# How the lower parts of the second MLP's weights are made: VectorE's subtraction, or ScalarE's negated copy and an accumulating DMA

## The chip, the cores and the metric

One core of one Trainium2 chip runs the whole program. The metric is the device time of one execution in microseconds (us). Before the change it is 1009.81 us, the median of 3 runs that lie between 1009.17 and 1010.68.

## The reference

A trunk of two layers runs over 512 tokens of width 1024, in float32. What matters here is its last part, the MLP of layer 1 and the final norm:

```
def squared_relu_mlp(h, w1, w2):          # w1: 1024 x 4096, w2: 4096 x 1024
    return jnp.square(jax.nn.relu(h @ w1)) @ w2

h = rms_norm(x, norm_w[1, 1]) * (1 + scale) + shift
x = x + gate * squared_relu_mlp(h, mlp_w1[1], mlp_w2[1])
return rms_norm(x, final_norm_w)
```

Everything ahead of it (attention and MLP of layer 0, the pooling mixer of layer 1) is the same before and after the change.

## The kernel before

Every matrix product is computed from split operands. A float32 matrix W is written as W = hi + lo: hi is W rounded to the type float32r, in which TensorE multiplies, and lo = W - hi is rounded to the same type. A product a @ W is then three matmuls into one PSUM bank: hi by hi, hi by lo, lo by hi. So each weight tile must be loaded, cast by ScalarE (tile `wh`, the upper part) and subtracted (tile `wl`, the lower part) before TensorE may use it. `mm3` (L368) multiplies in the order upper by upper, upper weight by lower activation, lower weight by upper activation; `product` (L1612) takes the lower weight second.

The last stage, from about 670 us on, computes the MLP of layer 1. It consists of two kinds of work on TensorE.

An up block (`up_blocks`, L449) makes 128 of the 4096 hidden columns for all 512 tokens: 24 matmuls of 128x512, about 5.6 us. Two neighbouring blocks share two weight tiles of 128x1024, one for the first four and one for the last four of the eight chunks of the inner dimension. These tiles are loaded by `load_w` (L340), which calls `load_hi` (L346): a DMA from SyncE's queue into a raw tile, the cast by ScalarE at L364, and the subtraction by VectorE at L366.

The down projection is done in Strassen's manner: the hidden columns come in four pairs of 512-column chunks, and for the first three pairs (class `Pair`, L1575) the product with the 2x2 blocks of w2 is replaced by seven products of half the size (`product`, L1612), each of 24 matmuls in two banks, about 5.5 us. Their weight operands are the blocks 11, 21, 22 and the differences T1 to T4, which `combine` (L1600) makes on VectorE in place, on top of the raw tiles of blocks that are split already. `split` (L1587) makes upper and lower parts of one operand: four times a cast of 128x512 by ScalarE (L1595) and a subtraction by VectorE (L1596), in two pairs of tiles of 1024 columns. The last pair is multiplied directly (`direct`, L1680), with four splits.

TensorE's instructions stand in the order written (`TE` is `_InOrder` in this stage). After the loop that starts at L1742 the order for each of the three pairs is: up blocks and product 1, more up blocks, products 2, 5 and 6, up block 0 of the next chunk, product 3, up block 1, product 7, up block 2, product 4, up block 3. The instructions of ScalarE, VectorE, GpSimd and SyncE are placed by a list scheduler, which simulates a timeline; each engine then executes its own in the order placed.

The tiles are few. The pool `wsplit` holds four `wh` and four `wl` tiles, thus the operands of two products; splits and the first two up blocks of a chunk (`pools[0]`) take turns in it. The pool `wsplit2` holds two of each for the last two up blocks of a chunk (`pools[1]`) and the split activations (`split_g`). A cast can start only when TensorE has done with the tile's old content, so the time from that release to the first use of the new content is all that cast and subtraction have. Raw tiles are freed, for the next load on SyncE's queue, when cast and subtraction have read them.

In this stage GpSimd executes nothing. Its queue can issue DMAs, as SyncE's does.

Of the kernel before, what the change touches and what calls it, by code (L numbers as in the profile page):

```python
# [11 lines left out]
F32 = mybir.dt.float32  # L12
# [3 lines left out]
ALU = mybir.AluOpType  # L16
# [68 lines left out]
def trunk(ctx: ExitStack, tc: tile.TileContext, ins, out):  # L85
    nc = tc.nc
    V, S, G, TE = nc.vector, nc.scalar, nc.gpsimd, nc.tensor
# [16 lines left out]
    def nm(s):  # L104
        uid[0] += 1
        return f"{s}_{uid[0]}"
# [71 lines left out]
    rt = wraw.tile([P, RAW], F32, tag="raw", name="rel")  # L178
# [153 lines left out]
    def load(dst, src):  # L332

        if isinstance(V, _InOrder):
            anchor[0] = Q.dma_start(dst, src)
        else:
            with tc.issue_after(anchor[0].ins):
                nc.sync.dma_start(dst, src)

    def load_w(src, a, b, parts=1, lo=V, pool=None):  # L340

        w, make_lo = load_hi(src, a, b, parts, pool)
        make_lo(lo)
        return w

    def load_hi(src, a, b, parts=1, pool=None):  # L346

        n = a * b
        rt = wraw.tile([P, RAW], F32, tag="raw", name=nm("w"))
        if parts == 1:  # L350
            load(rt[:, :n].rearrange("p (a b) -> p a b", a=a), src)
        else:
            dst = rt[:, :n].rearrange("p (a c b) -> p a c b", a=a, c=parts)
            for i in range(parts):
                load(dst[:, :, i], src[:, :, i])
        if pool is None:
            pool = wsplit
        if spare:
            turn[0] += 1
            if turn[0] % 6 >= 4:  # L360
                pool = spare[0]
        th = pool.tile([P, RAW], F32R, tag="wh", name=nm("wh"))
        tl = pool.tile([P, RAW], F32R, tag="wl", name=nm("wl"))
        S.copy(th[:, :n], rt[:, :n])  # L364
        w = tuple(t[:, :n].rearrange("p (a b) -> p a b", a=a) for t in (th, tl))
        return w, lambda e: e.tensor_tensor(tl[:, :n], rt[:, :n], th[:, :n].bitcast(F32), op=ALU.subtract)  # L366

    def mm3(ps, wh, wl, ah, al, start, stop):  # L368
# [8 lines left out]
    class Mlp:  # L377
# [51 lines left out]
        def load_first(self, fp, k0):  # L429
            self.first[fp, k0], lo = load_hi(self.w1[:, k0 : k0 + 4, 256 * fp : 256 * fp + 256], 4, 256)  # L430
            return lo
# [17 lines left out]
        def up_blocks(self, c, g, f0=0, pools=(None, None)):  # L449

            hh, hl = self.h
            for f in range(f0, 4):
                if f % 2 == 0:
                    by = []
                    for k0 in (0, 4):
                        c0 = c * FC + f * P
                        wh, wl = load_w(self.w1[:, k0 : k0 + 4, c0 : c0 + 256], 4, 256, pool=pools[f // 2])
                        by += [(wh, wl, i) for i in range(4)]
                ps = mm_ps()
                cs = slice(f % 2 * P, (f % 2 + 1) * P)  # L460
                for k in range(ND):
                    wh, wl, kk = by[k]
                    mm3(ps, wh[:, kk, cs], wl[:, kk, cs], hh[k], hl[k], k == 0, k == ND - 1)
                self.act(g, f, slice(0, T), ps)
                yield
# [8 lines left out]
        def down(self, c, g):  # L474
            gh, gl = g
            for j in range(ND):
                if j % 2 == 0:
                    wh, wl = load_w(self.w2[:, 4 * c : 4 * c + 4, j * P : j * P + 256], 4, 256)
                ps = mm_ps()
                cs = slice(j % 2 * P, (j % 2 + 1) * P)  # L480
                for f in range(4):
                    mm3(ps, wh[:, f, cs], wl[:, f, cs], gh[:, f], gl[:, f], f == 0, f == 3)
                x_update(j, ps, self.gate[:, j : j + 1])
# [111 lines left out]
    V, S, G, TE = [_InOrder(tc, e) for e in (V, S, G, TE)]  # L595
# [290 lines left out]
    class Attention(Steps):  # L886
# [61 lines left out]
        def load(self, key, src, a, b, parts=1):  # L948
            self.w[key], lo = load_hi(src, a, b, parts)
            yield  # L950
            lo(G)
            yield
# [383 lines left out]
    V, S, G, TE = nc.vector, nc.scalar, nc.gpsimd, nc.tensor  # L1336
# [187 lines left out]
    V, S, G, TE = [_InOrder(tc, e) for e in (V, S, G, TE)]  # L1524
# [13 lines left out]
    V, S, G, TE = nc.vector, nc.scalar, nc.gpsimd, nc.tensor  # L1538
# [12 lines left out]
    for tb in range(NT):  # L1551
        rt = wraw.tile([P, RAW], F32, tag="raw", name=nm("xT"))
# [22 lines left out]
    class Pair:  # L1575
# [11 lines left out]
        def split(self, key, pool=wsplit):  # L1587

            w = []
            for f in range(4):  # L1590
                if f % 2 == 0:
                    th = pool.tile([P, RAW], F32R, tag="wh", name=nm("wh"))
                    tl = pool.tile([P, RAW], F32R, tag="wl", name=nm("wl"))
                cs = slice(f % 2 * T, (f % 2 + 1) * T)
                S.copy(th[:, cs], self.raw[key, f])  # L1595
                V.tensor_tensor(tl[:, cs], self.raw[key, f], th[:, cs].bitcast(F32), op=ALU.subtract)  # L1596
                w.append((th[:, cs], tl[:, cs]))
            return w

# [136 lines left out]
                    V.tensor_tensor(t, p, q, op=op)  # L1736

    gs1 = mlp1.gs
    TE, pools = _InOrder(tc, nc.tensor), (wsplit, wsplit2)
    pair = Pair(0, gs1, True)  # L1740
    blocks = mlp1.up_blocks(1, gs1[1], 2, pools)
# [25 lines left out]
    V, weights = _InOrder(tc, nc.vector), []  # L1767
# [43 lines left out]
```

## Time and profile before

| | us |
|---|---|
| median of the three timed runs | 1009.81 |
| the profiled execution | 1007.54 |
| its span, from first to last instruction | 1005.8 |
| TensorE busy within the span | 972.7 |
| VectorE busy | 702.2 |
| ScalarE busy | 478.6 |
| GpSimd busy | 187.3 |
| mean granted TensorE clock, as a share of 2.4 GHz | 0.992 |

The engines appear as PE (TensorE), DVE (VectorE), ACT (ScalarE), POOL (GpSimd) and SP (SyncE). A line such as L366 is a line of the kernel; L81 is the helper that records instructions whose order is fixed, so there the tile names tell which instruction it is. An engine that is idle does no harm unless the engine that sets the end waits for it. For idle time, the name behind the arrow is the instruction whose end released the waiting one.

### The profile page before, as it was taken

The page shows a single profiled execution, that of the slowest core. Times are in us where ns is not written, and L with a number is a line of the kernel's source. Part 1 is how long each engine was busy: PE and PEld are TensorE (multiplying, and loading weights), DVE is VectorE, ACT ScalarE, POOL GpSimd, SP SyncE. Part 2 cuts the span into 40 slices and gives each one's busy share as a digit, 9 for nine tenths or more (in the row PEclk, how much of TensorE's full clock was granted, in tenths as well). Part 3 has the DMA queues.
Part 4 walks back from the last instruction along what each step waited for, and adds up shares of the span by engine and source line. Part 5 has one row for each costly group of instructions (what it writes and reads, how often), then busy time and mean ns, then how long its engine had stood idle before and what let it go on. Part 6 is the DMA issues. An engine that isn't in the chain of part 4 may idle for free.

```text
span 1005.8 us, 14329 instructions
## 1 busy us (share of the span) xinstructions
PE 972.7 (97%) x5392; PEld 808.6 (80%) x5392; DVE 702.2 (70%) x1192; ACT 478.6 (48%) x886; POOL 187.3 (19%) x136
## 2 busy tenths in 40 slices
PE   6989999998999999999999999899999999989996
PEld 5668888788978778777787999898788788778885
DVE  3679886657885766666574457869658966887485
ACT  6566656656542333334143435574664544344411
POOL 0043335466020111112022337200000000000000
PEclk9999999999999999999999999899999999999999
DMA  9963667542385646556575312181351243043212
GB/s 309 334 170 105 174 189 225 154 140 64 107 256 166 220 134 209 185 169 210 167 224 152 105 44 85 39 294 46 126 167 43 84 161 90 0 146 105 71 35 83
DMA packets 119367, 145.57 MB, mean 145 GB/s; under 512 B 5782, under 2 KB 86018, under 8 KB 119298
## 3 DMA queue, kind: packets, MB, share of 16 engines
q1 hardware_dynamic: 119138, 144.59, 46.4%
q8 instruction: 42, 0.69, 0.3%
q14 instruction: 27, 0.22, 0.1%
q10 hardware_dynamic: 160, 0.07, 0.0%
HBM read 140.25 MB, written 4.39 MB: 144 GB/s over the span
## 4 chain that ended last, share of the span: by engine, by line
PE 81%; DVE 8%; DMA 3%; issue 3%; ACT 2%; POOL 2%; SPq 1%; DVEq 0%; POOLq 0%; ACTq 0%
PE mm L81 32%; PE sc L81 10%; PE mm L370 9%; PE mm L372 9%; PE mm L371 9%; PE po L81 5%; PE tp L81 4%; DMA adaw<-in_ada_w 3%; PE ad L81 2%; DVE hl L81 1%; DVE wl L366 1%; DVE wl L1596 1%; SPq L81 1%; DVE sl L1609 1%; POOL wl L81 1%
## 5 line engine op out<-in xcount | busy, mean ns | idle before, releaser
L364 ACT CAST wh<-w 128x1024 fp32r<-128x1024 f32 x82 | 85.8, 1050 | 110.3 <-PE mm L371 80.5
L81 PE MATMUL mm<-hh,wl 128*128 128x512 f32 (+1 forms) x312 | 117.1, 383 | 4.3 <-DVE wl L366 4.3
L81 PE MATMUL mm<-hl,wh 128*128 128x512 f32 (+1 forms) x312 | 116.7, 381 | 1.6 <-DVE hl L81 1.6
L81 PE MATMUL mm<-hh,wh 128*128 128x512 f32 (+1 forms) x312 | 117.9, 385 | 0.0
L366 DVE TENSOR_TENSOR wl<-w,wh 128x1024 fp32r<-128x1024 f32 x76 | 100.0, 1322 | 23.5 <-ACT wh L364 22.3
L81 POOL TENSOR_TENSOR wl<-w,wh 128x1024 fp32r<-128x1024 f32 x36 | 88.1, 2456 | 77.9 <-ACT wh L81 75.1
L372 PE MATMUL mm<-hh,wl 128*128 128x512 f32 (+1 forms) x256 | 95.8, 375 | 0.0
L371 PE MATMUL mm<-hl,wh 128*128 128x512 f32 (+1 forms) x256 | 95.7, 375 | 0.0
L370 PE MATMUL mm<-hh,wh 128*128 128x512 f32 (+1 forms) x256 | 95.4, 377 | 0.0
L1595 ACT CAST wh<-w 128x512 fp32r<-128x512 f32 x100 | 56.9, 619 | 59.9 <-PE mm L81 24.4
L370 PE MATMUL mm<-gh,wh 128*128 128x512 f32 x192 | 76.0, 396 | 0.1
L371 PE MATMUL mm<-gl,wh 128*128 128x512 f32 x192 | 74.9, 390 | 0.0
L372 PE MATMUL mm<-gh,wl 128*128 128x512 f32 x192 | 74.9, 390 | 0.0
L81 PEld LDWEIGHTS mm<-hh,wl 128*128 128x128 f32 x312 | 59.8, 192 | 18.0 <-DVE wl L366 6.3
L395 ACT ACTIVATE r<-mm 128x512 f32<-128x512 f32 (+1 forms) x46 | 26.8, 583 | 93.5 <-PE mm L81 49.7
L81 PEld LDWEIGHTS mm<-hl,wh 128*128 128x128 f32 x312 | 59.9, 192 | 13.2 <-DVE hl L81 1.8
L81 PEld LDWEIGHTS mm<-hh,wh 128*128 128x128 f32 x312 | 59.9, 192 | 11.8 <-ACT wh L364 0.8
L1596 DVE TENSOR_TENSOR wl<-w,wh 128x512 fp32r<-128x512 f32 x84 | 54.1, 684 | 15.1 <-ACT wh L1595 15.1
L248 DVE SCALAR_TENSOR_TENSOR acc<-adaw,sc,acc 128x512 f32<-128x512 f32 x60 | 46.6, 777 | 20.7 <-DMA adaw<-in_ada_w 20.1
L274 POOL TENSOR_TENSOR adaw<-adaw 128x512 f32<-128x512 f32 x12 | 15.7, 1307 | 233.7 <-ACT adaw L272 225.8
L375 DVE SCALAR_TENSOR_TENSOR x<-mm,mod,x 128x512 f32<-128x512 f32 x48 | 35.6, 746 | 32.0 <-PE mm L372 31.7
L399 DVE TENSOR_TENSOR r<-r 128x512 f32<-128x512 f32 (+1 forms) x49 | 34.4, 703 | 31.5 <-ACT gh L396 31.5
(486 smaller groups left out, 2536.6 us busy)
## 6 DMA issues: line engine op xcount, KB each, us to landing
w<-in_mlp_w SPq DMA_DIRECT2D x98, 512.0 KB, 4.2
adaw<-in_ada_w SPq DMA_DIRECT2D x92, 512.0 KB, 4.6
w<-in_mlp_w SPq DMA_DIRECT2D x64, 256.0 KB, 3.7
w<-in_attn_w_in SPq DMA_DIRECT2D x8, 512.0 KB, 3.9
w<-in_attn_w_out SPq DMA_DIRECT2D x8, 512.0 KB, 3.6
w<-in_attn_w_in SPq DMA_DIRECT2D x8, 392.0 KB, 8.2
xin<-in_x SPq DMA_DIRECT2D x4, 512.0 KB, 5.8
adaw<-in_ada_w SPq DMA_DIRECT2D x8, 256.0 KB, 6.2
```

What stands on the lines that cost most here:

```text
L81: return lambda *args, **kw: self.tc.keep_in_program_order(f(*args, **kw))
L248: V.scalar_tensor_tensor(acc, rv, sk, acc, op0=ALU.mult, op1=ALU.add)
L364: S.copy(th[:, :n], rt[:, :n])
L366: return w, lambda e: e.tensor_tensor(tl[:, :n], rt[:, :n], th[:, :n].bitcast(F32), op=ALU.subtract)
L370: TE.matmul(ps, wh, ah, start=start, stop=False)
L371: TE.matmul(ps, wh, al, start=False, stop=False)
L372: TE.matmul(ps, wl, ah, start=False, stop=stop)
L375: V.scalar_tensor_tensor(x[j][:, ts], ps, g, x[j][:, ts], op0=ALU.mult, op1=ALU.add)
L395: S.activation(r, ps, AF.Relu)
L399: V.tensor_tensor(r, r, r, op=ALU.mult)
L1595: S.copy(th[:, cs], self.raw[key, f])
L1596: V.tensor_tensor(tl[:, cs], self.raw[key, f], th[:, cs].bitcast(F32), op=ALU.subtract)
```

## The change

From the last stage on, the lower part is made in two other steps. ScalarE writes the negated upper part into the lower part's tile (`S.mul` by -1), and a DMA issued from GpSimd's queue adds the raw tile onto it (`accum_op=ALU.add`): the DMA reads the raw tile and the lower tile, both in on-chip memory, and writes the lower tile. VectorE's subtraction at L366 and L1596 disappears there. This holds for the 26 weight tiles of the up blocks (128x1024, 512 KB each) and the 100 of the splits (128x512, 256 KB each). The splits of activations (`split_g`, `act_parts`) and all stages ahead keep their subtractions.

```
+    lo_by_dma = []
+
+    def subtract_by_dma(lo, raw, hi):
+
+        S.mul(lo, hi.bitcast(F32), -1.0)
+        G.dma_start(lo, raw, accum_op=ALU.add)
+
...
         w = tuple(t[:, :n].rearrange("p (a b) -> p a b", a=a) for t in (th, tl))
+        if lo_by_dma:
+            return w, lambda e: subtract_by_dma(tl[:, :n], rt[:, :n], th[:, :n])
         return w, lambda e: e.tensor_tensor(tl[:, :n], rt[:, :n], th[:, :n].bitcast(F32), op=ALU.subtract)
...
                 S.copy(th[:, cs], self.raw[key, f])
-                V.tensor_tensor(tl[:, cs], self.raw[key, f], th[:, cs].bitcast(F32), op=ALU.subtract)
+                subtract_by_dma(tl[:, cs], self.raw[key, f], th[:, cs])
                 w.append((th[:, cs], tl[:, cs]))
...
     gs1 = mlp1.gs
+    lo_by_dma.append(1)
     TE, pools = _InOrder(tc, nc.tensor), (wsplit, wsplit2)
```

## Rows read from the trace of the kernel before

**Rows 1.** The page's first part: each engine's busy time, its share, its instructions.

```profile
PE 972.7 (97%) x5392; PEld 808.6 (80%) x5392; DVE 702.2 (70%) x1192; ACT 478.6 (48%) x886; POOL 187.3 (19%) x136
```

**Rows 2.** Windows of the last stage: busy time by engine, granted clock, DMA share, GB/s.

```profile
670.00:755.00 85.00, 83.97 (x421) 70.38 (x421) 59.49 (x97) 50.77 (x89) 0.00 (x0) 1.00 0.42 133
755.00:925.00 170.00, 165.20 (x712) 132.68 (x711) 134.65 (x215) 76.14 (x117) 0.00 (x0) 1.00 0.30 93
```

**Rows 3.** What TensorE waited for from 670 us: total us, times, longest us.

```profile
PE mm L81 <- DVE wl L366: 4.3, 4, 2.2
PE mm L81 <- DVE gl L400: 1.5, 3, 0.5
```

**Rows 4.** ScalarE's instructions from 670 us by line and shape.

```profile
L1595 ACT CAST wh<-w 128x512 fp32r<-128x512 f32 x100 | 56.9, 619 | 59.9 <-PE mm L81 24.4 <-PE po L81 23.0 <-PE sc L81 11.7
L364 ACT CAST wh<-w 128x1024 fp32r<-128x1024 f32 x26 | 27.2, 1052 | 17.3 <-PE mm L81 9.0 <-PE po L81 4.4 <-issue 2.0
```

**Rows 5.** VectorE's instructions from 670 us by line and shape.

```profile
L1596 DVE TENSOR_TENSOR wl<-w,wh 128x512 fp32r<-128x512 f32 x84 | 54.1, 684 | 15.1 <-ACT wh L1595 15.1
L366 DVE TENSOR_TENSOR wl<-w,wh 128x1024 fp32r<-128x1024 f32 x26 | 31.5, 1219 | 9.9 <-ACT wh L364 9.9
```

**Rows 6.** The DMA issues: queue, count, KB each, median us from issue to landing.

```profile
w<-in_attn_w_in SPq DMA_DIRECT2D x8, 392.0 KB, 8.2
...
x_scratch<-xT SPq DMA_DIRECT2D x4, 512.0 KB, 2.9
...
out<-x SPq DMA_DIRECT2D x6, 256.0 KB, 2.0
bias<-bias_scratch SPq DMA_DIRECT2D x8, 128.0 KB, 6.3
```

**Rows 7.** The page's groups: GpSimd's subtraction of the same shape, earlier in the kernel.

```profile
L81 POOL TENSOR_TENSOR wl<-w,wh 128x1024 fp32r<-128x1024 f32 x36 | 88.1, 2456 | 77.9 <-ACT wh L81 75.1
```

**Rows 8.** ScalarE's timeline, five stretches: start, us, instruction, count, idle before and releaser.

```profile
708.20 1.14 ACT L1595 CAST wh<-w 128x512 fp32r<-128x512 f32 x2
...
716.62 1.05 ACT L364 CAST wh<-w 128x1024 fp32r<-128x1024 f32 x1 [0.82 <-PE sc L81]
...
719.14 1.05 ACT L364 CAST wh<-w 128x1024 fp32r<-128x1024 f32 x1
...
731.07 1.14 ACT L1595 CAST wh<-w 128x512 fp32r<-128x512 f32 x2
...
739.55 2.19 ACT L364 CAST wh<-w 128x1024 fp32r<-128x1024 f32 x2 [0.77 <-PE po L81]
...
886.58 1.06 ACT L364 CAST wh<-w 128x1024 fp32r<-128x1024 f32 x1 [0.79 <-PE sc L81]
```

**Rows 9.** TensorE's timeline, five stretches, same columns.

```profile
714.56 0.39 PE L81 MATMUL sc<-wl,sh 128*128 128x512 f32 x1
...
718.99 0.51 PE L81 MATMUL mm<-hh,wl 128*128 128x512 f32 x1 [0.53 <-DVE wl L366]
...
737.54 0.39 PE L81 MATMUL tp<-wl,sh 128*128 128x512 f32 x1
...
743.97 0.40 PE L81 MATMUL mm<-hh,wl 128*128 128x512 f32 x1
...
890.58 0.51 PE L81 MATMUL mm<-hh,wl 128*128 128x512 f32 x1 [2.15 <-DVE wl L366]
...
894.05 0.50 PE L81 MATMUL mm<-hh,wl 128*128 128x512 f32 x1 [0.42 <-DVE wl L366]
```

**Rows 10.** TensorE's timeline ahead of a spell at the lower clock.

```profile
230.62 0.70 PE L81 MATMUL ad<-sqsum,inv_d 128*128 128x256 f32 x2 [2.65 <-DVE mod L81]
```

**Rows 11.** Windows after that idle time, and in a shorter one late in the kernel.

```profile
231.30:234.80 3.50, 3.50 (x19) 3.50 (x18) 1.79 (x5) 2.21 (x6) 1.77 (x1) 0.51 0.19 32
...
890.60:894.00 3.40, 3.03 (x12) 2.16 (x12) 3.40 (x5) 0.00 (x0) 0.00 (x0) 1.00 0.53 156
```

## The prediction

> **What bounds the kernel now.** I read the page's engine line first. TensorE is busy 972.7 us, 97% of the span, VectorE 70% [rows 1]. The change touches the stage from 670 us on alone, so I read that stage by windows: TensorE is busy 83.97 of 85 and 165.20 of 170 us up to 925, at the full granted clock, while VectorE is busy 59.49 and 134.65, ScalarE 50.77 and 76.14, GpSimd not at all [rows 2]. So TensorE's instruction stream sets the end, and it is idle some 5.8 us in these 255. The list of its waits says for what: 4.3 us for the subtraction of the up blocks' weights (L366), 1.5 us for lower activations (L400), nothing else [rows 3]. All that a faster or an emptier VectorE can give back is therefore 5.8 us. What the change can take is larger, because it lengthens the way from a released weight tile to a lower part that is ready, and that way is already the one on which TensorE waits.
>
> **What goes and what comes.** VectorE loses 84 subtractions (54.1 us), 26 large ones (31.5 us) [rows 5] and 16 more of the small kind near the end (16 by 684 ns, 10.9 us): some 96 us of an engine that is not the bound. By itself I cost that at nothing; TensorE hides it. ScalarE gains as many instructions as it has casts there: 100 of 0.62 us and 26 of 1.05 us [rows 4], taking the multiplication to last as long as the cast of the same shape (two small ones in a row take 1.14 us, so they start 0.52 apart [rows 8]); the casts occupy 56.9 + 27.2 us, so some 84 us more. A third of that falls into the first window, which goes from 51 to about 79 of 85 us: nearly full, so its other work will queue there. I cost that queueing at 0 with an upper bound of 5 us. GpSimd's queue gains 126 DMAs, 39.8 MB, each behind a wait for ScalarE's multiplication; behind the waiting DMA stand only others of its kind, for which TensorE waits.
>
> The new step is the landing time of an accumulating DMA, L. No row shows one. The nearest: a plain store of 256 KB lands 2.0 us after issue, one of 512 KB after 2.9 us [rows 6], so 256 KB more cost 0.9 us and 1.1 are fixed. An accumulation reads two streams and writes one; I count its bytes twice: 1.1 + 2 x 0.9 = 2.9 us for 256 KB, 1.1 + 4 x 0.9 = 4.7 for 512 KB. What GpSimd spends on issuing one is not shown either: I bound it by 0 and by the 2.46 us that it takes to subtract such a tile itself [rows 7], and take the middle, 1.2. That makes L = 4.1 us (256 KB) and 5.9 us (512 KB). The bounds are 2.0 and 2.9 us below (as cheap as the plain stores) and 6.3 and 8.2 us above (the slowest DMAs of this kernel, smaller than these [rows 6]).
>
> The Trainium skill (DMA: Bandwidth & Descriptors, section on the anatomy of one DMA on the SWDGE path) gives for a DMA issued from GpSimd about 2.0 us plus bytes at 436 GB/s, an estimate of 2.6 and 3.2 us; and in Collectives: The Full Stack, section on the bandwidth ceiling, it says that a reduction halves the rate, since it needs two source reads and not because the addition costs cycles. With the bytes doubled the page's line gives 3.2 and 4.4 us, and the sum below would be some 26 us by it instead of 41; no row here shows a DMA from GpSimd, so neither is confirmed.
>
> Now place by place, where the released tile is used soon. **(a) Up block 0 after product 6, three times.** In the first pair the cast starts at 716.62 and ends at 717.67 [rows 8]; TensorE uses the lower part at 718.99, after waiting 0.53 us [rows 9]. After: cast end 717.67, multiplication to 718.72, landing at 724.6: 5.6 us later. The second tile's cast (719.14) slides by the inserted multiplication to 720.19, is negated by 722.3 and lands at 728.2; TensorE, resuming at 724.6, needs it twelve matmuls later (2.8 us), at 727.4: 0.8 us more. Together 6.4. In the third pair the cast ends at 887.64, the landing is at 894.6 where TensorE went on at 890.58, 4.0 us; its second wait of 0.42 us at 894.05 is replaced by one of about 0.3: 3.9. The middle pair lies between, 5.2. Sum 15.5 us.
>
> **(b) Up block 2, three times.** Its second tile is cast as the second of a burst that starts at 739.55 and ends at 741.74 [rows 8]; the lower part is used at 743.97 without a wait [rows 9]: 2.23 us of slack, and the same within 0.1 us in the other two pairs. Its own multiplication takes 1.05 of them, and that of the burst's first tile 0 to 1.05, depending on the order placed; 0.65 remain: 5.9 - 0.65 = 5.25 us each, 15.8 in all.
>
> **(c) Product 6 on T2, three times.** The fourth cast ends at 709.34 [rows 8]; with three multiplications ahead (3 x 0.52) and its own it is negated by 711.5 and lands at 715.6, by 0.5 later if GpSimd issues four in a row; TensorE wants it at 714.56 [rows 9]. That is 1.5 us; I take 1 in each pair, as the casts come some tenths earlier in the others: 3. **(d) Product 7 on T3, three times.** The fourth cast ends at 732.21 [rows 8]; ahead of it stand three small multiplications and a large one, so 735.4, landing 739.8 with the queue; wanted at 737.54 [rows 9]: 2.3 us, 2 per pair, 6. The last split, for block 22 near the end, is like (c): 1. The other splits and tiles are cast a whole product or more ahead of their use, and 24 matmuls of about 0.23 us, 5.5 us, hide most of L.
>
> Two waits move rather than arise. `combine` overwrites raw tiles in place, so on VectorE it now waits for the DMA that reads them; behind it in VectorE's order stand the differences and lower activations that TensorE wants a few us later. With 96 us freed I cost this at 0, bounded by 2 us a pair. SyncE's loads into such tiles are issued some 4 us later; they feed operands that are cast at least an up block later, so nothing.
>
> The direct sum is 15.5 + 15.8 + 3 + 6 + 1 = 41 us. **The clock.** After 2.65 us without a matmul [rows 10] the granted clock was 0.51 for the next 3.5 us, in which TensorE ran at 1.2 instead of 2.4 GHz; after the 2.15 us late in this stage [rows 9] it stayed at 1.00 [rows 11]. The six waits of (a) and (b) are 4 to 6 us long, above both. At half the rate for 3.5 us each loses 1.7 us: 10 us. If none of them drops the clock, 0. I take 10.
>
> The profiled execution took 1007.54 us, 2.3 below the median of the runs. 1007.5 + 41 + 10 = 1058.5; put at the median, 1061 us. With the lower bounds of L the places give 6.6 + 6.8 + 0.2 = 13.6 us and no clock spell: 1023. With the upper ones 22.5 + 22.7 + 9.5 + 12.5 + 3 = 70 us, and 20 of clock over twelve waits: 1100.
>
> **Rivals.** *The DMA is light.* Landings near 3 us, waits too short for the clock: 1023 to 1040. For it speak the 2.0 and 2.9 us of the stores, against it the second stream and GpSimd's part. The line of the Trainium skill's page DMA: Bandwidth & Descriptors, with the bytes counted once, would put it here (an estimate of some 16 us, 1026).
>
> *GpSimd's queue or the accumulation's rate becomes the bound.* If issuing one takes 2.5 us, the bound of rows 7, bursts of four stretch to 10 us: (a) 19.5, (b) 23.9, (c) three times 5.9, (d) three times 7.3, end 6, together 89, and 22 us of clock over thirteen waits: 1120. It decides from about 2.7 us per DMA on, when 126 of them fill the whole 336 us; beyond that the time grows without a limit that the trace shows. Against it: nothing else stands in that queue, and the 16 engines are busy only 42% and 30% of these windows [rows 2].
>
> *All of it is hidden and TensorE gains.* The wait on VectorE (5.8 us) goes and nothing replaces it: 1004. It decides where the landing takes less than the subtraction did, 1.2 us minus the added multiplication's 1.05, thus below about 0.2 us in (a) and 2.2 in (b); no DMA of the kernel lands that fast. Between, at L about 1.5 us, is no change.
>
> **How the numbers follow.** The forecast's case 0.60, the heavy queue 0.22, the light DMA 0.13, hidden or even 0.05 (0.03 faster, 0.02 the same). A measurement of this kernel can tell a difference of about 0.2%, 2 us. Slower: 0.60 + 0.22 + 0.13 = 0.95. The range reaches from the light case, 1025, to the heavy one, 1118, and leaves out what is lighter than the plain stores and a DMA rate below what any row shows.
>
> **What would show it.** Right: in the profile after, TensorE's longest waits are for DMAs into `wl`, at up blocks 0 and 2 with 4 to 6 us, at products 6 and 7 with 1 to 2; granted clock below 1.00 behind the long ones; VectorE's busy time down by about 96 us, ScalarE's up by 84; landings of the new DMAs near 4 and 6 us. Wrong: landings below 3 us or above 9, a GpSimd queue that is never idle, TensorE waiting for ScalarE or for `combine` instead, or a clock that stays at 1.00 through waits of 5 us.

## The result, and the profile after

The changed kernel takes 1115.31 us (median of 4 runs, 1113.89 to 1115.86) against 1009.49 (1007.59 to 1010.68): the ratio is 1.1046, with a 95% interval of 1.1026 to 1.1067. The forecast was 1061. The sign was right and the time lies in the range, but the loss is 106 us where 51.5 were forecast.

The page of the changed kernel: busy time and share, then two of the DMA queues (packets, MB, share of 16 engines), two groups of part 5, and the new DMAs in part 6 (KB each, median us from issue to landing).

```profile
PE 1002.1 (90%) x5392; PEld 823.2 (74%) x5392; DVE 614.4 (55%) x1066; ACT 553.1 (50%) x1012; POOL 296.2 (27%) x262
...
q1 hardware_dynamic: 119138, 144.59, 41.9%
q0 software_dynamic: 18144, 39.85, 20.3%
...
L345 POOL DMA_DIRECT2D wl<-w x126 | 108.8, 1037 | 318.8 <-ACT wl L344 249.9
...
L344 ACT ACTIVATE wl<-wh 128x512 fp32r<-128x512 f32 (+1 forms) x126 | 84.5, 713 | 0.2
...
wl<-w POOLq DMA_DIRECT2D x100, 256.0 KB, 5.4
...
wl<-w POOLq DMA_DIRECT2D x26, 512.0 KB, 7.0
```

Against [rows 1], TensorE's busy time rose by 29.4 us for the same 5392 matmuls; as its instructions are the same, that is the lower clock. VectorE lost 88 us (96 were forecast), ScalarE gained 74.5 on the page (84.5 in the new group itself; instructions in a row overlap by some 0.1 us, as two casts of 0.62 do in [rows 8]). The queue q0 holds the accumulating DMAs alone: 39.85 MB in 20.3% of 16 engines' 1113.2 us is 11.0 GB/s per engine; q1, which copies, moved 19.4.

What TensorE waited for from 670 us on (us in total, times, longest), which before came to 5.8 us in all [rows 3]:

```profile
PE mm L81 <- DMA wl<-w: 53.8, 7, 9.7
PE tp L81 <- DMA wl<-w: 14.5, 5, 4.9
PE sc L81 <- DMA wl<-w: 9.8, 12, 2.3
PE mm L81 <- DVE gl L409: 4.5, 3, 2.8
```

`mm` with `wl` are the up blocks, `tp` product 7, `sc` product 6. The sum, 82.6 us, less the 5.8 of before, is 76.8; with 29.4 us of slower matmuls it accounts for 106.2 of the 107.4 us by which the span grew. TensorE's own timeline of the changed kernel shows the places (start, duration, in brackets the idle time before and its releaser):

```profile
728.62 0.50 PE L81 MATMUL sc<-wl,sh 128*128 128x512 f32 x1 [2.26 <-DMA wl<-w]
741.65 0.80 PE L81 MATMUL mm<-hh,wl 128*128 128x512 f32 x1 [7.50 <-DMA wl<-w]
...
766.78 0.50 PE L81 MATMUL tp<-wl,sh 128*128 128x512 f32 x1 [4.69 <-DMA wl<-w]
...
859.72 0.79 PE L81 MATMUL mm<-hh,wl 128*128 128x512 f32 x1 [8.13 <-DMA wl<-w]
...
884.15 0.79 PE L81 MATMUL tp<-wl,sh 128*128 128x512 f32 x1 [4.91 <-DMA wl<-w]
...
902.40 0.79 PE L81 MATMUL mm<-hh,wl 128*128 128x512 f32 x1 [7.73 <-DMA wl<-w]
```

These are the four places of the prediction. Behind the up blocks' waits the first matmul lasts 0.80 us where it lasted 0.40 to 0.51 [rows 9]; behind the two waits of 2.26 and 4.69 us it still lasts 0.50. In all, the waits of the three pairs are: up block 0 7.50 + 8.13 + 8.76 = 24.4 us (4.3 of them were there before [rows 3]), up block 2 9.65 + 7.73 + 8.54 = 25.9, product 7 14.5, product 6 8.7; the splits near the end wait 1.1. Two that the prediction did not have are 3.5 at the first up block of the stage (from 687.6) and 3.0 more for lower activations.

Windows of the changed kernel (length; busy PE, PEld (TensorE's weight loads), DVE, ACT, POOL; granted clock, DMA share, GB/s): the two of [rows 2], two bursts of lower parts, and the first matmuls of up block 0 behind its wait.

```profile
670.00:755.00 85.00, 67.67 (x316) 55.12 (x315) 29.29 (x52) 48.99 (x88) 20.94 (x24) 0.88 0.75 171
755.00:925.00 170.00, 131.05 (x510) 101.74 (x509) 45.59 (x76) 91.64 (x147) 46.45 (x54) 0.89 0.81 178
...
755.50:785.70 30.20, 15.74 (x60) 11.61 (x58) 0.42 (x1) 17.25 (x28) 10.31 (x12) 0.87 1.01 223
...
838.70:859.70 21.00, 10.31 (x41) 6.81 (x39) 6.56 (x8) 11.61 (x17) 8.61 (x10) 0.91 1.01 226
...
742.00:744.00 2.00, 2.00 (x6) 1.52 (x6) 0.00 (x0) 0.00 (x0) 0.00 (x0) 0.50 0.97 226
```

The column to look at is the last but one, the DMA share. Before, the 16 DMA engines were busy 42% and 30% of these windows [rows 2]; now 75% and 81%, and in the bursts they are full (1.01). GpSimd, which issues, is busy 34% and 41% of a burst: the engines are the limit, not the issuing. The records of one burst, the one behind product 2 of the second pair (GpSimd's DMAs alone, all of 256 KB, us):

```
issued    landed    issue to landing
838.75    842.08    3.33
839.29    843.60    4.31
839.88    845.21    5.34
840.41    847.57    7.15
842.55    849.65    7.10
844.02    851.72    7.70
845.58    853.31    7.73
846.12    855.40    9.28
```

Issues are some 0.5 us apart in the first four, landings 1.5 to 2.4; from 842.22 on, SyncE's loads (256 KB, landing after 5.6 to 7.5) lie between them. Of all 100 small DMAs the shortest landing is 3.28 us, the median 5.4; of the 26 large ones 4.55 and 7.0. Sixteen of the 126 land after more than 9 us, which the prediction had named as a sign of being wrong.

### The profile page after: what moved, and what is told of

Read it like the earlier page. It is cut to its first block, busy times and chain, and to the rows that moved or that the text cites. A ratio compares the mean times of both kernels' runs of the same rounds, so it can differ in the third digit from the quotient of the medians.

```text
span 1113.2 us, 14667 instructions
## 1 busy us (share of the span) xinstructions
PE 1002.1 (90%) x5392; PEld 823.2 (74%) x5392; DVE 614.4 (55%) x1066; ACT 553.1 (50%) x1012; POOL 296.2 (27%) x262
## 3 DMA queue, kind: packets, MB, share of 16 engines
q0 software_dynamic: 18144, 39.85, 20.3%
## 4 chain that ended last, share of the span: by engine, by line
PE 58%; DMA 16%; issue 12%; DVE 7%; POOL 4%; ACT 2%; SPq 0%; POOLq 0%; DVEq 0%; ACTq 0%
PE mm L81 22%; DMA wl<-w 10%; PE mm L379 7%; PE mm L381 7%; PE mm L380 7%; PE sc L81 6%; DMA adaw<-in_ada_w 3%; PE po L81 3%; PE tp L81 3%; POOL wl L345 2%; DMA w<-in_mlp_w 2%; PE ad L81 2%; DVE hl L81 1%; DVE wl L375 1%; ACT wh L371 1%
## 5 line engine op out<-in xcount | busy, mean ns | idle before, releaser
L345 POOL DMA_DIRECT2D wl<-w x126 | 108.8, 1037 | 318.8 <-ACT wl L344 249.9
L81 PE MATMUL mm<-hh,wl 128*128 128x512 f32 (+1 forms) x312 | 123.5, 403 | 53.8 <-DMA wl<-w 53.8
L81 PE MATMUL mm<-hl,wh 128*128 128x512 f32 (+1 forms) x312 | 121.3, 396 | 1.6 <-DVE hl L81 1.6
L81 PE MATMUL mm<-hh,wh 128*128 128x512 f32 (+1 forms) x312 | 122.3, 399 | 0.0
L81 PEld LDWEIGHTS mm<-hh,wl 128*128 128x128 f32 x312 | 63.2, 202 | 69.4 <-DMA wl<-w 56.8
L381 PE MATMUL mm<-hh,wl 128*128 128x512 f32 (+1 forms) x256 | 95.8, 375 | 0.0
L380 PE MATMUL mm<-hl,wh 128*128 128x512 f32 (+1 forms) x256 | 95.7, 375 | 0.0
L379 PE MATMUL mm<-hh,wh 128*128 128x512 f32 (+1 forms) x256 | 95.4, 377 | 0.0
L344 ACT ACTIVATE wl<-wh 128x512 fp32r<-128x512 f32 (+1 forms) x126 | 84.5, 713 | 0.2
L274 POOL TENSOR_TENSOR adaw<-adaw 128x512 f32<-128x512 f32 x12 | 15.7, 1307 | 234.1 <-ACT adaw L272 169.1
L404 ACT ACTIVATE r<-mm 128x512 f32<-128x512 f32 (+1 forms) x46 | 26.9, 585 | 99.6 <-PE mm L81 57.2
L375 DVE TENSOR_TENSOR wl<-w,wh 128x1024 fp32r<-128x1024 f32 x50 | 67.2, 1350 | 15.1 <-ACT wh L371 14.0
L81 PEld LDWEIGHTS mm<-hl,wh 128*128 128x128 f32 x312 | 62.8, 201 | 14.4 <-DVE hl L81 1.8
L81 PEld LDWEIGHTS mm<-hh,wh 128*128 128x128 f32 x312 | 63.1, 202 | 12.4 <-ACT wh L371 0.4
L1604 ACT CAST wh<-w 128x512 fp32r<-128x512 f32 x100 | 56.9, 618 | 25.9 <-PE mm L81 13.6
```

The lines of the kernel that those rows point to most:

```text
L81: return lambda *args, **kw: self.tc.keep_in_program_order(f(*args, **kw))
L344: S.mul(lo, hi.bitcast(F32), -1.0)
L345: G.dma_start(lo, raw, accum_op=ALU.add)
L379: TE.matmul(ps, wh, ah, start=start, stop=False)
L380: TE.matmul(ps, wh, al, start=False, stop=False)
L381: TE.matmul(ps, wl, ah, start=False, stop=stop)
```

## The experiments

Theory A: an accumulating DMA by itself lands soon enough, but each occupies the DMA engines for about 1.5 us per 256 KB, so those of a burst queue behind each other and with SyncE's loads. Rival B: ScalarE's 84 us of multiplications, and where they come in its order, make the lower parts late. Rival C: each DMA's own landing time is the cost. Diffs are against the changed kernel unless another is named. For scale, with what TensorE waited in all from 670 us on and its busy time there: 5.8 and 321.7 us before, 82.6 and 352.1 after.

**The multiplication without the DMA.** VectorE adds the raw tile onto the negated part.

```
-        G.dma_start(lo, raw, accum_op=ALU.add)
+        V.tensor_tensor(lo, raw, lo.bitcast(F32), op=ALU.add)
```

> ScalarE's negated copy stays, and VectorE adds the raw tile onto it; no DMA is issued from GpSimd. Theory A (the accumulating DMAs queue behind each other: 1.5 us per 256 KB after the first) and theory C (each DMA's own landing time) both give back nearly all: 1010 to 1016 us, the rest being the added multiplication ahead of up block 0. Theory B (ScalarE's 84 us of multiplications and their place in its order) keeps most of the 106 us: above 1060.

1045.58 us, ratio 1.0361 (1.033 to 1.0392). Both forecasts missed. TensorE's waits in it:

```profile
PE mm L81 <- DVE wl L345: 20.3, 6, 4.1
PE mm L81 <- DVE wl L81: 7.6, 1, 7.6
PE mm L81 <- DVE gl L409: 3.2, 3, 2.2
PE mm L81 <- ACT wh L371: 1.2, 1, 1.2
```

The six of the first line are up blocks 0 and 2: 3.4 us each without any DMA, so a multiplication on the way costs more there than its 1.05 us. The 7.6 us are a place that the changed kernel does not have (behind the third pair VectorE's order is fixed, and its additions wait for multiplications there). So B has a share: 36 of 106 us in this kernel, 7.6 of them at a place of its own.

**The two halves of the change.** First only the 26 tiles of the up blocks by DMA, then only the 100 splits.

```
-                subtract_by_dma(tl[:, cs], self.raw[key, f], th[:, cs])
+                V.tensor_tensor(tl[:, cs], self.raw[key, f], th[:, cs].bitcast(F32), op=ALU.subtract)
```

> Only the 26 tiles of the up blocks take the DMA; the 100 splits go back to VectorE. A: the large DMAs land alone (5.8 us), waits of 18 us at up block 0 and 20 us at up block 2, clock 18: about 1060. C: about 1050. B: in proportion to the multiplications, 27 of 84 us: 1043.

1059.06 us, ratio 1.0493 (1.0465 to 1.0522).

```
-    lo_by_dma.append(1)
```

> Only the 100 splits take the DMA; the up blocks' tiles go back to VectorE. A: waits of 8 us at product 6, 9 at product 7, 4.5 for lower activations, clock 7: about 1035, and the excesses of this run and of the one with the up blocks alone add to some 77 us, well below 106. C: the two excesses add to 106. B: 1075.

1040.04 us, ratio 1.0292 (1.0262 to 1.0322). The waits of the first kernel, then of the second:

```profile
PE mm L81 <- DMA wl<-w: 39.3, 7, 6.5
PE mm L81 <- DVE gl L409: 1.5, 3, 0.5
```

```profile
PE sc L81 <- DMA wl<-w: 9.4, 12, 1.8
PE tp L81 <- DMA wl<-w: 8.3, 9, 1.9
PE mm L81 <- DVE gl L409: 4.3, 3, 2.8
PE mm L81 <- DVE wl L375: 1.3, 3, 0.5
```

Alone, the up blocks wait 6.1 to 6.5 us in all six places and product 7 waits 8.3 us instead of 14.5. The losses of 49.6 and 30.6 us add up to 80; together they are 106. Some 26 us exist only where both halves run at once (about 3 of them because either half alone also takes away most of VectorE's 4.3 us of [rows 3], which can be taken away only once). That speaks against C. Whether it is A or B, the records of the DMAs for which TensorE waits at the six up blocks tell. From the cast's end to the DMA's issue it takes 2.83 us in the mean with the up blocks alone and 2.84 in the changed kernel; from issue to landing it takes 4.98 us and 7.09. So at the up blocks the added 2.1 us per wait are the landings, which is A. At product 7 both grow, by 0.8 and 0.6 us for the DMA that ends the longest wait of each pair, so there B has a part.

**The splits of T4 left to VectorE.** They are issued just ahead of up block 2's tiles.

```
-                subtract_by_dma(tl[:, cs], self.raw[key, f], th[:, cs])
+                if key == "T4":
+                    V.tensor_tensor(tl[:, cs], self.raw[key, f], th[:, cs].bitcast(F32), op=ALU.subtract)
+                else:
+                    subtract_by_dma(tl[:, cs], self.raw[key, f], th[:, cs])
```

> As the changed kernel, but the 12 splits of T4 are made by VectorE. A: these four stand straight ahead of up block 2's tile in the DMA engines; its waits fall from 25.9 us to about 15, and the time to about 1098. C: nothing lands earlier, 1113 to 1115. B: four multiplications less ahead of that tile, 2 us a pair: 1108.

1114.09 us, ratio 1.1023 (1.0973 to 1.1073): A's time missed, C's met, though not as C meant it. A's mechanism holds at the place (the DMAs for which up block 2 waits land after 5.0 to 5.5 us instead of 6.9 to 8.3, and its waits fell from 25.9 to 18.9 us, 6.3 each, as in the kernel with the up blocks alone), but product 7 waited 17.2 us instead of 14.5; in the first pair four of SyncE's loads now go out between 758.39 and 760.57, beside T3's DMAs. Here, taking 12 of 126 out of a full queue let others in. In the profiled execution all waits are 77.5 us, 5 fewer than in the changed kernel, which the spread of the four runs (1107.56 to 1117.51) hides.

**The same DMAs without the addition.** They copy the raw tile into the lower part's; the lower parts are not subtracted here.

```
-        G.dma_start(lo, raw, accum_op=ALU.add)
+        G.dma_start(lo, raw)
```

> The same DMAs without the addition: each copies the raw tile over the lower tile, after the same multiplication (so the lower parts are not subtracted). A: 256 KB take about 0.9 us of the engines instead of 1.5, the queues of four shorten by 2 to 3 us; waits fall from 78 us to about 50, time about 1075. C with the cost in GpSimd's issue and the fixed landing: a lone DMA still lands after 3.3 us and the time stays above 1105.

1068.17 us, ratio 1.0579 (1.0544 to 1.0614); TensorE waits 46.9 us, as A said. Its queue of copies and its waits:

```profile
q0 software_dynamic: 18144, 39.85, 11.7%
...
PE mm L81 <- DMA wl<-w: 37.2, 6, 7.1
PE tp L81 <- DMA wl<-w: 6.0, 3, 2.4
PE mm L81 <- DVE gl L409: 2.2, 3, 1.2
PE sc L81 <- DMA wl<-w: 1.5, 2, 1.0
```

The same packets and bytes take 11.7% of 16 engines' 1060.2 us, 20.1 GB/s per engine, where with the addition they took 20.3% of a longer span, 11.0. By itself a copied 256 KB lands after 2.25 us, 512 KB after 2.87 (accumulated: 3.28 and 4.49, the latter in the kernel with the up blocks alone). Accumulating instead of copying thus costs 47 us of the 106; part of it may be GpSimd's issue, which takes 0.53 us for a copy and 1.04 in the mean for an accumulation. The products' waits shrink, but the up blocks still wait 5.7 to 7.1 us each: there the way from the cast's end to the issue takes 2.2 to 3.7 us, and the copy, behind others in flight, 4.1 to 5.4.

**ScalarE's multiplications beside everything.** The kernel before, with the added multiplications into a PSUM bank that nobody reads (diff against before, the call sites as in the change).

```
+        for q in range(lo.shape[1] // T):
+            S.mul(lo_by_dma[0], hi[:, q * T:(q + 1) * T].bitcast(F32), -1.0)
+        V.tensor_tensor(lo, raw, hi.bitcast(F32), op=ALU.subtract)
...
+    lo_by_dma.append(ad_ps())
```

> The kernel before, VectorE's subtractions and all, with ScalarE's 126 added multiplications alone, written into a PSUM bank that nobody reads (the 26 large ones as two of 128x512 each); nothing waits for a multiplication but what stands behind it on ScalarE. This measures the queueing on ScalarE that the prediction costed at 0, with a bound of 5 us. The prediction's value: 1010 to 1015 us. B (ScalarE's work and its order have a large share by themselves): 1030 to 1045 us, with TensorE waiting for upper parts or for lower ones whose casts came late.

1020.53 us, ratio 1.0111 (1.009 to 1.0131): between both forecasts. Its waits:

```profile
PE mm L81 <- DVE wl L81: 7.0, 1, 7.0
PE mm L81 <- DVE wl L346: 4.9, 4, 2.1
PE mm L81 <- DVE gl L410: 1.5, 3, 0.5
```

The 7.0 us are the place behind the third pair again. The other two lines are those of [rows 3] plus 0.6 us: within the pairs, 91 us more on ScalarE cost next to nothing as long as nothing waits for them.

**The negation taken from the raw tile, ahead of the cast,** in the whole change and with the up blocks alone; the multiplication then does not wait for the cast.

```
-        S.mul(lo, hi.bitcast(F32), -1.0)
...
+        if lo_by_dma:
+            S.mul(tl[:, :n], rt[:, :n], -1.0)
         S.copy(th[:, :n], rt[:, :n])
...
+                S.mul(tl[:, cs], self.raw[key, f], -1.0)
```

> The negated upper part is rounded from the raw tile itself, ahead of the cast, so cast and DMA run side by side. A and C: each waiting place gains a cast, 1.05 us at up blocks 0 and 2, 0.6 to 2 at products 6 and 7: some 12 us of waits, 1100. B (the place of the multiplication in ScalarE's order, 1 to 3.5 us behind its cast): 25 us of waits and 8 of clock, 1080.

1094.44 us, ratio 1.0846 (1.0821 to 1.0872), nearer to the 1100 of A and C than to B's 1080. Product 7's waits nearly vanish (14.5 to 1.9 us), but up block 2 now waits 12.2 to 12.7 in each pair: the two blocks together last 26.9 us in the mean, where they lasted 29.2. From product 7 to the end of up block 2 the landings set the pace, whichever operand goes first.

> e_up (the 26 up-block tiles alone by DMA, 1059 us), with the negation made ahead of the cast, from the raw tile, so that the DMA does not wait for the multiplication's place in ScalarE's order. B (ScalarE's order has a real share): the waits at the up blocks, 6.2 us each in e_up, fall to about 4, time about 1044. C (the landing time of the lone DMA alone sets the wait): 1055 to 1059.

1056.03 us, ratio 1.047 (1.0446 to 1.0495). C's time, but not as C meant it: up block 0's waits fell from 6.1 to 3.1 to 4.8, as B said, and up block 2's rose from 6.3 to 8.2 to 9.2. In the first pair three large DMAs now go out at 746.99, 749.83 and 751.32; the last, for which TensorE waits, lands 8.17 us later.

**TensorE kept busy.** Idle matmuls (26, 26 and 14) ahead of up block 0, up block 2 and product 7, 46 us in all.

```
+    def warm(n):
+        ps = ad_ps()
+        for _ in range(n):
+            TE.matmul(ps, h1[0][0][:, 0:P], h1[1][0], start=True, stop=True)
```

> The changed kernel with idle work for TensorE: 26 matmuls of 128x512 ahead of up blocks 0 and 2 and 14 ahead of product 7, in each of three pairs, into an unused bank (46 us in all, shorter than the 64.5 us of waits there). If the lower clock behind the waits is a cost of its own (29 us of longer matmuls), it goes down to about 8 and the time to about 1095. If the landings set the pace and the slow matmuls lie beside them, the time stays at 1113 to 1118.

1115.13 us, ratio 1.1036 (1.0987 to 1.1084). The time at half clock fell from 81.9 to 41.0 us and the kernel did not get faster by anything that shows. Product 7 and up block 2 with their fills take 29.6, 29.8 and 28.8 us, without fills 29.9, 29.4 and 28.4: the slow matmuls lie beside DMAs that are late anyway.

**Where there is slack: block 22.** It is used by product 3 and cast some 13 us ahead of that: product 6 and up block 0 lie between. First all its splits by DMA, then those in the pairs alone, then those in the pairs on GpSimd as a plain instruction (diffs of the call in `split`, all else as before).

```
+                if key == "22":
+                    subtract_by_dma(tl[:, cs], self.raw[key, f], th[:, cs])
+                else:
                     V.tensor_tensor(...)
...
+                if key == "22" and not isinstance(V, _InOrder):
+                    subtract_by_dma(tl[:, cs], self.raw[key, f], th[:, cs])
...
+                e = G if key == "22" and not isinstance(V, _InOrder) else V
+                e.tensor_tensor(tl[:, cs], self.raw[key, f], th[:, cs].bitcast(F32), op=ALU.subtract)
```

> Only the splits of block 22 take the DMA (12 in the pairs, 4 at the end): they are cast a product ahead of use, no later difference overwrites their raw tile, and on VectorE they stand ahead of the subtraction for up block 0. A and C: no wait for them except at the end (1 us), VectorE's part of the wait at up block 0 goes (2.4 us): 1007 to 1010. B: four multiplications ahead of up block 0's cast cost 2 us a pair: 1014.

1009.11 us, ratio 1.000 (0.9982 to 1.0018). VectorE's 4.3 us fell to 1.6, a new wait of 1.1 came at the end of the kernel.

> Block 22's twelve splits inside the three pairs by accumulating DMA, the four at the end of the kernel left to VectorE. A (a DMA that has a product's slack and no neighbour in the queue costs nothing): the 4.3 us that TensorE waited for VectorE's lower parts [rows 3] fall to about 1.6, the 1.1 us wait of e_22 at the end is gone, 1006 to 1007 us, ratio 0.997 to 0.999. B (the multiplications on ScalarE cost what the DMA saves): 1009 or more, with new waits for ScalarE's upper parts or the gate's lower parts.

1005.45 us (12 runs; before 1009.52 in 23), ratio 0.9973 (0.9957 to 0.9988): faster than both kernels, by 2.7 us at the ratio. Its waits:

```profile
PE mm L81 <- DVE wl L375: 1.6, 3, 0.5
PE mm L81 <- DVE gl L409: 1.5, 3, 0.5
PE mm L81 <- ACT wh L371: 0.4, 1, 0.4
```

They are 2.3 us fewer than in [rows 3], which is the gain within its interval. The twelve DMAs land after 3.7 to 6.3 us, and nobody waits.

> The same twelve splits of block 22, subtracted on GpSimd as an ordinary instruction, with no DMA and no added multiplication on ScalarE. A (what costs is the path through negation and DMA; a free engine costs nothing): like e_22b, 1005 to 1007 us, VectorE's lower-part wait of 4.3 us falls below 2. Rival (GpSimd and VectorE hinder each other at the tiles): VectorE's instructions beside it grow longer and the time is 1010 us or more.

1012.48 us (12 runs, 1007.37 to 1013.36), ratio 1.0013 (0.9996 to 1.0029): no gain, the rival's side. GpSimd's group, VectorE's lower activations beside it, and the same group in the kernel before:

```profile
L1597 POOL TENSOR_TENSOR wl<-w,wh 128x512 fp32r<-128x512 f32 x12 | 23.0, 1943 | 211.3 <-ACT wh L1595 211.3
...
L1610 DVE TENSOR_TENSOR sl<-z,sh 128x1024 fp32r<-128x1024 f32 x6 | 9.2, 1540 | 3.7 <-ACT sh L1609 3.7
...
L1609 DVE TENSOR_TENSOR sl<-z,sh 128x1024 fp32r<-128x1024 f32 x6 | 7.3, 1219 | 1.2 <-ACT sh L1608 1.2
```

Of VectorE's 38 subtractions of this shape the six that run while GpSimd subtracts last 1.77 us in the mean, the other 32 1.22. The wait for the up blocks' lower parts is 5.3 us there, not below 4.3.

## Why the prediction was wrong in size

**Right:** what bounds the kernel, that an emptier VectorE gives nothing back, the four places and the direction on every engine. The landing of a DMA by itself was near: 4.1 and 5.9 us taken, 3.3 and 4.5 the shortest, so too long by 0.8 and 1.4 us. The kernel with the up blocks alone took 1059 us, close to the forecast of 1061, but that is luck: 10 us of the 1061 are for splits that this kernel leaves to VectorE. At its up blocks 0 and 2 the waits grew by 33.2 us (37.5 less the 4.3 of before) where (a) and (b) say 31.3, from landings 0.9 us shorter than taken and a way to the issue 1.5 us longer; and the clock took 15.7 us where it was 10.

The Trainium skill (DMA: Bandwidth & Descriptors, the anatomy of one DMA on the SWDGE path) gave an estimate of 2.6 and 3.2 us for a DMA from GpSimd; the plain copies here took 2.25 and 2.87 at the shortest, and the accumulating ones 3.28 and 4.49, near the 3.2 and 4.4 that came out with the bytes doubled. For copies by themselves the page's estimate lies 0.3 to 0.4 us above the measurement.

**The step that failed** is the one from L to the places: the prediction used the landing time of a DMA by itself, with 0.5 us for a row of four ("by 0.5 later if GpSimd issues four in a row", and (d)'s "landing 739.8 with the queue"). Followers of a burst land 1.5 us or more apart, because the 16 engines are full; the fourth of the burst above landed 5.5 us behind the first, and the eighth took 9.28. The prediction took the engines' share in the windows of before (42% and 30%) as room, instead of adding the new bytes at their own, slower rate. The waits grew by (a) 20.1 us for 15.5, (b) 25.9 for 15.8, (c) 8.7 for 3 and (d) 14.5 for 6, some 29 us more than forecast at the four places. The DMA that ends the longest wait of each pair shows on which part of the way (us, means of three; forecast in brackets):

| | cast's end to issue | issue to landing |
|---|---|---|
| (a) up block 0 | 2.68 (1.05) | 6.48 (5.9) |
| (b) up block 2 | 3.00 (1.58) | 7.70 (5.9) |
| (c) product 6 | 2.49 (2.2) | 7.41 (4.6) |
| (d) product 7 | 2.99 (3.2) | 6.38 (4.4) |

Over three pairs the landings are 21 us longer than forecast and the way to the issue 9 to 10, so two thirds of the miss at these places are the queue in the DMA engines, and one third, almost all of it at the up blocks, is ScalarE's order.

The rival of the accumulation's rate had this mechanism at 0.22, and its 1120 us is the nearest of the four times, but it put the price in GpSimd's issuing (2.5 us each); an issue takes 1.0 us and the engines were the limit. Its point of decision, 126 DMAs filling 336 us, was the second error: a queue need not be full over the stage to hurt, bursts of 20 us are enough. This is shown by the landings that grew when both halves ran together, and by the rates of 11.0 and 20.1 GB/s with the 47 us between accumulating and copying.

**Costed at nothing.** ScalarE's queueing (0, bound 5 us): where nothing waits for the multiplications it cost 0.6 us within the pairs. On the path it cost more than its bound: the 9 to 10 us of the table. With VectorE adding, the six waits are 3.4 us each. At up block 0 of the first pair the cast ends at 732.49 and its multiplication starts at 734.45, behind a cast that waits for TensorE (ScalarE's timeline, columns as above):

```profile
731.44 1.05 ACT L371 CAST wh<-w 128x1024 fp32r<-128x1024 f32 x1 [1.47 <-PE sc L81]
733.49 1.05 ACT L1617 CAST sh<-gf 128x1024 fp32r<-128x1024 f32 x1 [1.01 <-PE sc L81]
734.45 1.05 ACT L344 ACTIVATE wl<-wh 128x1024 fp32r<-128x1024 f32 x1
```

`combine`'s wait (0, bound 2 us a pair): VectorE did wait, 41.2 us for the DMAs that read its raw tiles, but lower activations came later by 3.0 us in all, most of it in the first pair. Its group, in the list of VectorE's instructions from 670 us on:

```profile
L1611 DVE TENSOR_TENSOR w<-w,w 128x512 f32<-128x512 f32 x48 | 32.0, 690 | 43.0 <-DMA wl<-w 41.2 <-ACT wh L1604 1.1 <-ACT gp L425 0.2
```

SyncE's loads, "so nothing": their landing went from 3.2 to 6.4 us (256 KB, median of this stage), and where they lie between the accumulating DMAs of the burst above, those land up to 2.4 us apart instead of 1.5.

**The clock** cost 29 us of TensorE's busy time for 10: six spells of 3.5 us at half clock were forecast, and the trace has 82 us of them up to the last product of the pairs. It did not prove a cost of its own: with half of the slow time gone, the kernel took as long, and the 1095 us that such a cost would have given lies outside the interval. Where the DMAs set the pace, the slow matmuls lie beside late landings: at a faster clock TensorE would wait longer instead. In a profile the two add up, but taking away the one does not give it back.

**Open:** how the 106 us divide exactly between queue, addition and ScalarE's order. Measured one by one, multiplication on the path +36 (7.6 of waiting at a place of its own), the same with plain DMAs +59, with accumulating ones +106; the parts overlap, and the order of ScalarE differs in each.

## What to carry to other kernels

Price a moved step twice, by itself and in its burst: bytes divided by the rate of that kind of transfer, on engines that other queues use at the same moment; a mean share of 30 or 40% says nothing about the 20 us in which all of it comes. An operation taken from an engine that is not the bound may only go where its result has slack: the same DMA that cost 106 us everywhere gained 2.7 us for the one operand that is made a product and an up block ahead.

## What the runs showed of the hardware

An accumulating DMA between two tiles of on-chip memory moved 11.0 GB/s per DMA engine, where a plain copy between the same tiles from the same queue moved 20.1, a ratio of 0.55; the kernel's loads and stores moved 19.4. With the up blocks alone, whose DMAs take 7.4% of the engines, the rate is 10.9, so it does not come from the crowding. The rule of the Trainium skill that a reduction halves the rate because of its two source reads (Collectives: The Full Stack, the bandwidth ceiling) fits that roughly; no run here separates the second read from the addition. Issuing one kept GpSimd 0.84 us when alone and 1.04 in the mean, issuing a copy 0.53. GpSimd's own subtraction of 128x512 took 1943 ns in the mean, and VectorE's 128x1024 subtractions that ran beside it 1.77 us instead of 1.22.
